# A hybrid decoder trunk on one core: the second mixer's output projection, its combines, and three shifts of order around the norms

## The chip, the core and the metric

The kernel runs on one core of a Trainium2 chip. A core has a matrix engine (TensorE, PE below), a vector engine (VectorE, DVE), an engine for activation functions (ScalarE, ACT), a general engine (GpSimd, POOL) and a queue that issues most DMA transfers (SyncE, SP). Each takes its own instructions in its own order; semaphores tie them together. The metric is the device time in microseconds (us), the median over runs. Before the change it is 2555.88 us (three runs, 2554.9 to 2557.5).

## The reference

One sequence of 1024 tokens with 1024 channels passes two layers in fp32. Each layer adds a token mixer and a SwiGLU feed-forward block to the residual stream `h`, each behind an RMS norm. Layer 0 has gated DeltaNet heads and a short convolution, layer 1 has HGRN2 heads and dilated window attention:

```
for layer in range(DEPTH):                      # DEPTH = 2
    hn = rms_norm(h, norm_mix_g[layer])
    h = h + (mixer_ab if layer % 2 == 0 else mixer_cd)(hn, ...)
    hn = rms_norm(h, norm_ffn_g[layer])
    h = h + swiglu(hn, w_gate, w_up, w_down)
return rms_norm(h, norm_final_g)

# in mixer_cd: three windows (128, 512, 2048) with dilations 1, 4, 16, four heads of 128
for p, (window, dilation) in enumerate(SWA_PATTERNS):
    o_p, lse_p = dilated_window_attention(sq[:, :, p], sk[:, :, p], sv[:, :, p], window, dilation)
wts = softmax(stack(lses), axis=-1)             # over the three windows
o_d = einsum('bthpd,bthp->bthd', stack(outs), wts)
return concatenate([o_c, o_d], axis=-1) @ w_out # 512 HGRN2 channels, 512 attention channels
```

The outputs of the three windows are weighed by a softmax over their log-sum-exps and added (the combine); together with the HGRN2 channels they go through the output projection `w_out`, 1024 by 1024.

## The kernel before

The residual and all activations lie with channels on the 128 partitions and tokens along the free axis, in two halves of 512 tokens, so a tensor of 1024 channels is 8 tiles of 128x512 per half. A product in fp32 is three matmuls: each operand is split into a high part and a remainder (`split`, lines 100 to 103: a cast on ACT, then a subtraction on DVE), and `mm3` (lines 122 to 129) adds high times high (L127), and the two mixed products (L128, L129). An output tile over 8 channel tiles k thus takes 24 matmuls of 512 columns.

Weights are read in units of 128x1024 by `wload`: a DMA into a raw buffer (`raw`, two of them), then the split into one of four units (`ring`, tag `w`). PSUM has three sets of banks: two under `psg`, three under `psu`, three under `psm`.

`out_proj` (from line 1258) is the output projection of one half. It reads the eight tiles of the concatenated mixer output from DRAM (`cat`, into `cin`), splits them, and then computes eight outputs d in pairs: two weights are loaded, one output goes to `psu`, the other to `psg`, over all k in a given order. For layer 1 that order is 0, 1, 2, 4, 5, 6, 3, 7: the last of the HGRN2 tiles and of the attention heads come last. Each output is added to the residual (L1274), squared for the next norm (`piece`: ACT square at L184, sum `acc` on POOL at L188), and stored.

The class `Trunk` holds the norm. `sums` (L200) adds the squares over partitions by small matmuls with a tile of constants; the result `rows` is taken to SBUF by DVE (L203); `inverse` transposes it on PE (L208), DVE copies it (`v`, L210), POOL raises it to the power -1/2 (`r`, L215). `spread` (L239) brings it to all partitions by transposes, and `scale` (L249) multiplies. `rms` is `sums` followed by `inverse`.

The attention part of `mixer_cd` works through four heads and, for each, three windows. The outputs of windows 1 and 2 go to DRAM (`scr_o`); with the third comes `combine` (from line 2274) for a head and a half: it fetches the two tiles (`cm0`, `cm1`, one buffer each), works out the weights on DVE with one exponential on ACT (L2285 to L2296), multiplies each of the three tiles on ACT in four pieces by a per-token weight (L2300), adds on DVE (L2302), and, two steps later, transposes the sum on PE (L2307) into `psu`; a copy on ACT and a DMA take it to `cat`, tile 4 + head. The last head's tile for a half is the projection's operand k=7.

`Local` is layer 1's input projection, with products over sums and differences of channel and token halves. `early` prepares its first weights, `turn` runs the second half's norm while the first products run; `prepared` makes the high part of a weight at once and gives back a function that makes the low part (L312, L313). `silu2` (L783 to L787) computes SiLU with a tanh on ACT and one DVE instruction, and a store follows through `out`; `self.adds` is a queue of closures for DVE, which `flush` runs a step later.

In the main loop, `out_proj` runs as a generator for half 0 and half 1. In half 1, after the second output (d == 1), `tr.rms(0)` forms half 0's norm, and after the third `norm_first` applies it.

Some sections are written under a manual schedule, in which the order in the code is the order on the engines. Elsewhere the Tile scheduler orders instructions by priority, which follows the order of the code, and by estimated readiness; `tc.high_priority(offset=n)` moves an instruction up by n. So an edit there can shift other instructions on each engine too.

Of the kernel before, what the change touches and what calls it, by code (L numbers as in the profile page):

```python
# [16 lines left out]
MULT, ADD, SUB, MAX, MIN = ALU.mult, ALU.add, ALU.subtract, ALU.max, ALU.min  # L17

P = 128
T_LEN = 1024  # L20
DM = 1024
KT = DM // P
# [33 lines left out]
def hybrid_trunk_kernel(ctx: ExitStack, tc: tile.TileContext, x_t, w_all, w_down, w_ba, vecs, c_f, c_i, c_rope, out):  # L56
    nc = tc.nc
    V, S, G, T = nc.vector, nc.scalar, nc.gpsimd, nc.tensor
# [31 lines left out]
    def psg():  # L90
        return ps.tile([P, HT], F32, tag="g", name="psg", bufs=2)

    def psu():
        return ps.tile([P, HT], F32, tag="u", name="psu", bufs=3)
# [5 lines left out]
    def split(hi, lo, src, eng=V):  # L100

        S.copy(hi, src)  # L102
        eng.tensor_tensor(lo, src, hi.bitcast(F32), op=SUB)  # L103

    def unit():

        return ring.tile([P, 2, DM], F32R, tag="w", name="w", bufs=4)

    def wload(*names, ahead=0):

        us = []
        for n in names:
            us.append(unit())
            raw = ring.tile([P, DM], F32, tag="raw", name="raw", bufs=2)
            with tc.high_priority(offset=ahead):
                dma(raw, w_all[W_AT[n]])
            split(us[-1][:, 0, :], us[-1][:, 1, :], raw)
        return us

    def wk(w, i):  # L120

        return tuple(w[i][:, z, :].rearrange("p (k c) -> p k c", k=KT) for z in range(2))
# [8 lines left out]
    def hk(hn, z, k):  # L131

        return hn[k // KH][z][:, k % KH, :]

    def proj(w, hn, order=range(KT), o=None, first=True, last=True):
        o = psu() if o is None else o
        mm3(o, [(w[0][:, k, :], w[1][:, k, :], hk(hn, 0, k), hk(hn, 1, k)) for k in order], first, last)
        return o
# [604 lines left out]
    class Local(Up):  # L743
# [36 lines left out]
        def turned(self, f):  # L780
            return PAIRS[f][0] is not None

        def silu2(self, d, x):  # L783

            th = self.right.tile([P, HT], F32, tag="sw", name="th", bufs=2)
            S.activation(th, x, AF.Tanh, scale=0.5)
            V.scalar_tensor_tensor(d, th, 1.0, x, op0=ADD, op1=MULT)  # L787

        def bounds(self):

# [74 lines left out]
        def add22(self, f):  # L865
            c = self.c22.pop(f)
            if self.turned(f):
                b = self.c22[f] = psm()
                V.tensor_tensor(b, c, self.z[f], op=ADD)
            else:  # L870
                V.tensor_tensor(c, c, self.z[f], op=ADD)
                self.silu2(c, c)
                self.out(f, 1, 1, c)

        def rope22(self, f):
            if f in self.c22:
# [21 lines left out]
        def rope21(self, f):  # L898
            x = self.x.pop(f)
            if self.turned(f):  # L900
                self.rope(f, 1, 0, x)
            else:
                z = self.right.tile([P, HT], F32, tag="z", name="z", bufs=3)
                self.silu2(z, x)
                self.out(f, 1, 0, z)
                self.flush()

        def end12(self, f, b22):
            self.prod(self.z[f], f, "s4", b22, first=False)
# [100 lines left out]
        def early(self, hx):  # L1010

            def sub(eng, dst, x, y):
                eng.tensor_tensor(dst, x, y, op=SUB)

            xa = hx.tile([P, 2, DM], F32, tag="hn", name="xa", bufs=6)
            xu = hx.tile([P, 2, DM], F32R, tag="hn", name="xu", bufs=6)
            u0, g0 = (ring.tile([P, DM], F32, tag="raw", name="raw", bufs=2) for _ in range(2))
            dma(g0, self.source("g", 0))
            for i, kind in enumerate("gu"):
                dma(xa[:, i, :], self.source(kind, 1))  # L1020
            dma(u0, self.source("u", 0))
            w2 = self.raw("g", 2, True)
            ga, sa = xa[:, 0, :], xa[:, 1, :]
            self.part_a(0, g0)
            self.part_a(1, ga)
            V.tensor_tensor(sa[:, HT:], sa[:, :HT], sa[:, HT:], op=ADD)
            sub(V, sa[:, :HT], sa[:, HT:], ga[:, :HT])
            split(xu[:, 0, :], xu[:, 1, :], sa)
            self.named(1, xu, "s2", "s1")
            self.part_a(2, w2)  # L1030
            s = self.sums(g0, u0)
            sub(G, u0[:, :HT], g0[:, :HT], u0[:, :HT])
            sub(G, g0[:, HT:], g0[:, HT:], s[:, :HT])
            low = self.prepared(0, s, "s2", "s1")
            self.begun = ga, sa, w2, u0, g0, low

        def turn(self, tr, row, b11, b21, hx, close, left, right):

            def sub(eng, dst, x, y):
                eng.tensor_tensor(dst, x, y, op=SUB)  # L1040

            ga, sa, w2, u0, g0, low = self.begun
            self.p1(0, b11)
            parts = tr.sums(1)
            y = self.y[0] = psg()
            self.prod(y, 0, "a12", b21, last=False, ks=(0,))
            dg = tr.inverse(*parts)
            low()
            self.prod(y, 0, "a12", b21, first=False, ks=(1, 2, 3))
            pb = tr.spread(dg)  # L1050
            self.p1(1, b11)
# [29 lines left out]
            low = self.prepared(0, u0, "s3", "a22")  # L1081
# [8 lines left out]
            low = self.prepared(0, g0, None, "s4")  # L1090
# [14 lines left out]
            low = self.prepared(2, sa, "s2", "s1")  # L1105
# [7 lines left out]
            low = self.prepared(1, u1, "s3", "a22")  # L1113
# [21 lines left out]
            low = self.prepared(1, s, None, "s4", us)  # L1135
# [13 lines left out]
            self.end12(1, b22)  # L1149
            self.add12(1)  # L1150
            self.s = self.sums(a, b)
            while self.stores:
                self.flush()
            self.p7(2, t3)
            self.a, self.b = a, b
# [104 lines left out]
    def out_proj(name, cat_d, tr, src, order, half, hp):  # L1260
        qs = {}
        for k in order:
            if k // KH not in qs:
                qs[k // KH] = quarter()
            f = hp.tile([P, HT], F32, tag="m", name="cin", bufs=4 - layer)
            dma(f, cat_d[k])
            split(hk(qs, 0, k), hk(qs, 1, k), f)
        tr.begin(half, src)
        for d0 in range(0, KT, 2):
            w = wload((name, d0), (name, d0 + 1))  # L1270
            for i in range(2):
                o = proj(wk(w, i), qs, order, psg() if i else psu())
                h = tr.at(half, d0 + i)
                V.tensor_tensor(h, h, o, op=ADD)  # L1274
                tr.piece(half, d0 + i, alone=half == 1)
                tr.save(half, d0 + i, hd[2 * layer][half])
                yield
# [606 lines left out]
    def mixer_cd(hn, hp, qkd, wv):  # L1884
# [6 lines left out]
        with ExitStack() as es:  # L1891
# [382 lines left out]
            def combine(h, g, ol, sums):  # L2274

                t, st = [ol], [sums]
                for p in range(2):
                    a = tl(f"cm{p}", (4, 132))
                    dma(a[:, :, 0:P + 2],
                        scr_o[h, p, g * HT:(g + 1) * HT].rearrange("(j i) d -> i j d", i=P)[:, :, 0:P + 2])  # L2280
                    t.append(a)
                    st.append(a[:, :, P:P + 2])
                yield
                mx, dn, w3, tmp = tl("mx", (4,)), tl("dn", (4,)), tl("w3", (3, 4)), tl("tmp4", (4,))
                V.tensor_tensor(mx, st[0][:, :, 0], st[1][:, :, 0], op=MIN)  # L2285
                V.tensor_tensor(mx, mx, st[2][:, :, 0], op=MIN)
                for p in range(3):
                    V.tensor_tensor(w3[:, p, :], st[p][:, :, 0], mx, op=SUB)
                S.activation(w3, w3, AF.Exp, scale=-1.0)
                for p in range(3):  # L2290
                    d = dn if p == 0 else tmp
                    V.tensor_tensor(d, w3[:, p, :], st[p][:, :, 1], op=MULT)
                    if p:
                        V.tensor_tensor(dn, dn, tmp, op=ADD)
                V.reciprocal(tmp, dn)
                V.tensor_tensor(w3, w3, tmp[:, None, :].to_broadcast([P, 3, 4]), op=MULT)  # L2296
                for p in range(3):
                    for j in range(4):
                        x, w = t[p][:, j, 0:P], w3[:, p, j:j + 1]
                        S.activation(x, x, AF.Copy, scale=w)  # L2300
                    if p:
                        V.tensor_tensor(ol[:, :, 0:P], ol[:, :, 0:P], t[p][:, :, 0:P], op=ADD)  # L2302
                yield
                yield
                o = psu()
                for j in range(4):
                    T.transpose(o[:, j * P:(j + 1) * P], t[0][:, j, 0:P], ident)  # L2307
                go = tl("sw", bufs=2)
                S.copy(go, o)
                dma(catd[g][4 + h], go)  # L2310
# [86 lines left out]
    tr = Trunk(es)  # L2397
# [64 lines left out]
    first = [[u], []]  # L2462
# [35 lines left out]
    for layer in range(2):  # L2498
# [14 lines left out]
        tr = Trunk(es)  # L2513
        row = R_FFN + layer * KT
        for half in range(NH):
            steps = out_proj(("abo", "cdo")[layer], cat[layer][half], tr, residual[half],
                             ((4, 5, 6, 7, 0, 1, 2, 3), (0, 1, 2, 4, 5, 6, 3, 7))[layer], half, hp)
            for d, _ in enumerate(steps):
                if half == 1 and d == 1:
                    dg = tr.rms(0)  # L2520
                if half == 1 and d == 2:
                    b1 = norm_first(tr, row, dg)
        mes.close()
# [11 lines left out]
        with ExitStack() as fes:  # L2535
            tr = Trunk(es)
# [98 lines left out]
```

## Time and profile before

| | |
|---|---|
| median of three runs | 2555.88 us |
| profiled execution, whole | 2557.52 us |
| its span in the trace | 2555.5 us |
| mean granted PE clock | 0.996 |
| PE busy | 2516.3 us, 98% |
| DVE busy | 1694.8 us, 66% |
| ACT busy | 1088.6 us, 43% |
| POOL busy | 651.1 us, 25% |
| moved by DMA | 451.48 MB, 177 GB/s |

The profile comes from one execution. Busy time is the time in which an engine has an instruction in work; PE's matmuls overlap, so the count of starts in a stretch says more of PE than its busy time. The granted clock is 1.00 where PE runs at its full rate. A row of the timeline reads: start in the span, duration, engine, line, operation, output and inputs with their shapes, count, and in brackets the idle time of the engine before it with what ended it. The places of the change lie as follows in the span: layer 0's output projection around 420 to 520 us, layer 1's input projection from about 1110, the last attention heads and layer 1's output projection between 1740 and 1960 us.

### The profile page before, as it was taken

Reading aid. Unit: us, or ns where it says so; the run is one execution under the profiler, and the core shown is the slowest. Engines: PE = TensorE matmul, PEld = TensorE weight load, DVE = VectorE, ACT = ScalarE, POOL = GpSimd, SP = SyncE. Lnnn points to the kernel's source line nnn. Section 1 sums busy time; section 2 is a strip of 40 time slices with the busy share of each in tenths; the row PEclk is TensorE's granted clock in tenths of the full one; section 3 lists DMA queues with packets and bytes.
Section 4 is the critical chain, followed back from the end, with each engine's and each line's share of the span. In section 5 each row is a group of like instructions: output and inputs, shape, how many; then the busy total and the mean of one; then the engine's idle time right before and its main releaser. Section 6 shows DMA issues by size and latency. Waiting matters only on the chain.

```text
span 2555.5 us, 37524 instructions
## 1 busy us (share of the span) xinstructions
PE 2516.3 (98%) x13957; PEld 2086.8 (82%) x13957; DVE 1694.8 (66%) x2849; ACT 1088.6 (43%) x1859; POOL 651.1 (25%) x557
## 2 busy tenths in 40 slices
PE   9999999999999999999999999999899999999998
PEld 7888888888888888878888888878778888888887
DVE  8887786685655565568787765666568565666554
ACT  5422113443333344334676534456634333334442
POOL 0111111343333300033566310000033433330001
PEclk9999999999999999999999999999999999999999
DMA  4435457235556688633344544576652455668853
GB/s 158 156 120 167 129 159 258 106 102 183 182 189 215 204 302 276 197 128 132 128 142 148 184 132 139 154 204 192 197 173 87 165 190 188 201 219 284 279 175 124
DMA packets 281174, 451.48 MB, mean 177 GB/s; under 512 B 49152, under 2 KB 137760, under 8 KB 280736
## 3 DMA queue, kind: packets, MB, share of 16 engines
q1 hardware_dynamic: 280992, 449.10, 53.7%
q8 instruction: 109, 1.79, 0.3%
q14 instruction: 73, 0.60, 0.1%
HBM read 304.74 MB, written 144.26 MB: 176 GB/s over the span
## 4 chain that ended last, share of the span: by engine, by line
PE 80%; DVE 7%; ACT 3%; DMA 2%; issue 2%; POOL 1%; SPq 0%; DVEq 0%; POOLq 0%; ACTq 0%
PE psu L127 15%; PE psu L129 15%; PE psu L128 15%; PE psg L129 6%; PE psg L127 6%; PE psg L128 6%; PE psm L127 4%; PE psm L129 4%; PE psm L128 4%; DVE h L249 1%; PE psm L2247 1%; DMA cm<-scr_o 1%; DVE w L103 1%; DVE h L616 1%; DVE w L313 1%
## 5 line engine op out<-in xcount | busy, mean ns | idle before, releaser
L103 DVE TENSOR_TENSOR w<-raw,w 128x1024 fp32r<-128x1024 f32 x323 | 384.6, 1192 | 133.0 <-ACT w L102 132.4
L102 ACT CAST w<-raw 128x1024 fp32r<-128x1024 f32 x323 | 309.1, 958 | 266.1 <-PE psu L129 130.6
L127 PE MATMUL psu<-hnh,w 128*128 128x512 f32 x832 | 331.2, 398 | 0.2 <-ACT w L102 0.2
L129 PE MATMUL psu<-hnh,w 128*128 128x512 f32 x832 | 325.3, 391 | 0.5 <-DVE w L103 0.5
L128 PE MATMUL psu<-hnl,w 128*128 128x512 f32 x832 | 324.9, 390 | 0.0
L188 POOL TENSOR_TENSOR acc<-acc,sq 128x512 f32<-128x512 f32 x52 | 79.2, 1523 | 535.1 <-ACT sq L184 535.0
L129 PEld LDWEIGHTS psu<-hnh,w 128*128 128x128 f32 x832 | 156.3, 188 | 34.0 <-DVE w L103 1.0
L127 PEld LDWEIGHTS psu<-hnh,w 128*128 128x128 f32 x832 | 156.6, 188 | 32.9 <-ACT w L102 0.7
L128 PEld LDWEIGHTS psu<-hnl,w 128*128 128x128 f32 x832 | 156.7, 188 | 30.8
L326 POOL TENSOR_TENSOR ws<-raw 128x512 f32<-128x512 f32 x54 | 73.2, 1356 | 398.2 <-DMA raw<-in_dram 274.7
L103 DVE TENSOR_TENSOR w<-ws,w 128x1024 fp32r<-128x1024 f32 x51 | 66.7, 1309 | 119.8 <-ACT w L102 119.8
L103 DVE TENSOR_TENSOR hidq<-hr,hidq 128x1024 fp32r<-128x1024 f32 x72 | 82.0, 1141 | 78.4 <-ACT hidq L102 78.2
L102 ACT CAST hidq<-hr 128x1024 fp32r<-128x1024 f32 x72 | 70.3, 980 | 104.2 <-DMA hr<-ts 63.4
L127 PE MATMUL psm<-hidq,w 128*128 128x512 f32 (+1 forms) x275 | 106.1, 386 | 0.0
L128 PE MATMUL psm<-hidq,w 128*128 128x512 f32 (+1 forms) x275 | 105.8, 385 | 0.0
L129 PE MATMUL psm<-hidq,w 128*128 128x512 f32 (+1 forms) x275 | 105.8, 385 | 0.0
L846 POOL TENSOR_TENSOR sw<-sw,rope 128x512 f32<-128x512 f32 x48 | 71.7, 1493 | 93.5 <-ACT sw L845 60.3
L127 PE MATMUL psu<-t3h,w 128*128 128x512 f32 x240 | 93.9, 391 | 0.9 <-ACT u L389 0.9
L127 PE MATMUL psu<-t4h,w 128*128 128x512 f32 x240 | 93.7, 391 | 0.6 <-ACT c L396 0.6
L417 POOL TENSOR_TENSOR hid<-hid,c 128x512 f32<-128x512 f32 x44 | 62.1, 1411 | 125.1 <-ACT hid L416 124.9
L332 POOL TENSOR_TENSOR raw<-raw,ws 128x512 f32<-128x512 f32 x51 | 78.9, 1547 | 58.7 <-DVE w L103 57.5
L129 PE MATMUL psu<-t4h,w 128*128 128x512 f32 x240 | 93.4, 389 | 0.0
(536 smaller groups left out, 6702.6 us busy)
## 6 DMA issues: line engine op xcount, KB each, us to landing
raw<-in_dram SPq DMA_DIRECT2D x227, 512.0 KB, 4.1
sd<-in_dram SPq DMA_DIRECT2D x44, 512.0 KB, 3.8
hid<-hid SPq DMA_DIRECT2D x88, 256.0 KB, 2.9
sd<-sd SPq DMA_DIRECT2D x44, 512.0 KB, 3.1
hr<-ts SPq DMA_DIRECT2D x40, 512.0 KB, 4.5
raw<-sd SPq DMA_DIRECT2D x40, 512.0 KB, 4.5
qk<-z SPq DMA_DIRECT2D x52, 256.0 KB, 2.5
hd<-h SPq DMA_DIRECT2D x48, 256.0 KB, 2.9
```

The costliest lines, as they stand in the source:

```text
L102: S.copy(hi, src)
L103: eng.tensor_tensor(lo, src, hi.bitcast(F32), op=SUB)
L127: T.matmul(o, lh, rh, start=first and i == 0, stop=False, **kw)
L128: T.matmul(o, lh, rl, start=False, stop=False, **kw)
L129: T.matmul(o, ll, rh, start=False, stop=last and i == n - 1, **kw)
L188: (eng or G).tensor_tensor(a, a, q, op=ADD)
L249: V.scalar_tensor_tensor(h, h, vec[:, row + k:row + k + 1], pb, op0=MULT, op1=MULT)
L313: later(lambda: V.tensor_tensor(u[:, 1, c], src[:, c], u[:, 0, c].bitcast(F32), op=SUB))
L326: G.tensor_tensor(s[:, HT:], b[:, :HT], b[:, HT:], op=ADD)
L332: G.tensor_tensor(a[:, HT:], a[:, HT:], s[:, :HT], op=SUB)
L417: G.tensor_tensor(h, h, self.c22.pop(f), op=MULT)
L846: G.tensor_tensor(sw, sw, self.table[:, 1, t], op=MULT)
```

## The change

There are five edits.

A. `out_proj`: for layer 1 and half 0 the first four outputs are opened at once. Four weights are loaded, the four outputs run over the first seven k in two `psu` and two `psg` banks, and then each is closed with k=7. The other outputs, and the other halves, go in pairs as before.

B. `Local.early` and `turn`: of the second and third weight (f = 1, 2) only the high part is made in `early`; their low parts on DVE stand, with a third one that stood there already, behind the inverse of the second half's norm sums.

C. Main loop: `tr.rms(0)` runs with priority raised by 60, in both layers. In the resulting order the sums of half 0 (L200) stand behind 10 matmuls of half 1 in layer 0 and behind 9 in layer 1, where they stood behind 48; the transpose of the rows stands 3 matmuls behind them, the spread where it stood.

D. `combine`: the tile `ol` is scaled by one DVE instruction of 128x512 with the weights broadcast, in place of four ACT activations; the two additions come after it. The two fetched tiles are scaled on ACT as before.

E. `Local.silu2`: the DVE instruction after the tanh and its store go into the queue `self.adds` and so run a step later.

Line numbers after the change are higher by 3 at `silu2`, by 7 at the projection's addition (L1281) and by 7 or 8 in `combine` (the additions L2310, the scaling of `ol` L2308, the transposes L2315).

```diff
@@ silu2
-        def silu2(self, d, x):
+        def silu2(self, f, half, d, x):
             th = self.right.tile([P, HT], F32, tag="sw", name="th", bufs=2)
             S.activation(th, x, AF.Tanh, scale=0.5)
-            V.scalar_tensor_tensor(d, th, 1.0, x, op0=ADD, op1=MULT)
+            self.flush()
+            def add():
+                V.scalar_tensor_tensor(d, th, 1.0, x, op0=ADD, op1=MULT)
+                self.out(f, 1, half, d)
+            self.adds.append(add)
...
@@ early
-            self.part_a(1, ga)
+            low1 = self.prepared(1, ga, "a11", "a12")
...
-            self.part_a(2, w2)
+            low2 = self.prepared(2, w2, "a11", "a12")
...
-            self.begun = ga, sa, w2, u0, g0, low
+            self.begun = ga, sa, w2, u0, g0, (low1, low, low2)
@@ turn
             dg = tr.inverse(*parts)
-            low()
+            for low in lows:
+                low()
@@ out_proj
-        for d0 in range(0, KT, 2):
-            w = wload((name, d0), (name, d0 + 1))
-            for i in range(2):
-                o = proj(wk(w, i), qs, order, psg() if i else psu())
+        for d0, n in ((0, 4), (4, 2), (6, 2)) if layer and not half else ((0, 2), (2, 2), (4, 2), (6, 2)):
+            w = wload(*((name, d0 + i) for i in range(n)))
+            os_ = [None] * n
+            if n == 4:
+                os_ = [proj(wk(w, i), qs, order[:7], psg() if i % 2 else psu(), last=False) for i in range(n)]
+            for i, o in enumerate(os_):
+                o = proj(wk(w, i), qs, order[7 * (n // 4):], o or (psg() if i else psu()), first=n < 4)
@@ combine
-                for p in range(3):
+                for p in range(1, 3):
                     for j in range(4):
                         x, w = t[p][:, j, 0:P], w3[:, p, j:j + 1]
                         S.activation(x, x, AF.Copy, scale=w)
-                    if p:
-                        V.tensor_tensor(ol[:, :, 0:P], ol[:, :, 0:P], t[p][:, :, 0:P], op=ADD)
+                V.tensor_tensor(ol[:, :, 0:P], ol[:, :, 0:P], w3[:, 0, :, None].to_broadcast([P, 4, P]), op=MULT)
+                for p in range(1, 3):
+                    V.tensor_tensor(ol[:, :, 0:P], ol[:, :, 0:P], t[p][:, :, 0:P], op=ADD)
@@ main loop
                 if half == 1 and d == 1:
-                    dg = tr.rms(0)
+                    with tc.high_priority(offset=60):
+                        dg = tr.rms(0)
```

More of the change, by code (lines that the diff above doesn't have):

```diff
@@ L871, in add22 @@
                 V.tensor_tensor(c, c, self.z[f], op=ADD)
-                self.silu2(c, c)
-                self.out(f, 1, 1, c)
+                self.silu2(f, 1, c, c)
         def rope22(self, f):
@@ L903, in rope21 @@
                 z = self.right.tile([P, HT], F32, tag="z", name="z", bufs=3)
-                self.silu2(z, x)
-                self.out(f, 1, 0, z)
-                self.flush()
+                self.silu2(f, 0, z, x)
         def end12(self, f, b22):
@@ L1040, in sub @@
                 eng.tensor_tensor(dst, x, y, op=SUB)
-            ga, sa, w2, u0, g0, low = self.begun
+            ga, sa, w2, u0, g0, lows = self.begun
             self.p1(0, b11)
@@ L1151, in turn @@
             self.s = self.sums(a, b)
-            while self.stores:
+            while self.stores or self.adds:
                 self.flush()
```

## The prediction

> **What bounds the kernel now.** I read the page's totals first, then the busy time by stretches, then what TensorE (PE) waited for, and last the timeline round each place that the change touches.
>
> ```profile
> span 2555.5 us, 37524 instructions
> ```
> ```profile
> PE 2516.3 (98%) x13957; PEld 2086.8 (82%) x13957; DVE 1694.8 (66%) x2849; ACT 1088.6 (43%) x1859; POOL 651.1 (25%) x557
> ```
> ```profile
> 1860.00:1960.00 100.00, 96.58 (x443) 77.26 (x442) 76.83 (x81) 46.42 (x56) 33.38 (x18) 1.00 0.34 110
> 1960.00:2500.00 540.00, 540.00 (x2384) 447.30 (x2383) 319.77 (x392) 207.20 (x268) 144.39 (x106) 1.00 0.62 211
> 1826.70:1830.10 3.40, 3.37 (x11) 2.88 (x12) 2.00 (x4) 1.60 (x3) 0.00 (x0) 0.56 0.39 128
> 1137.10:1140.50 3.40, 3.40 (x11) 2.54 (x10) 0.94 (x1) 0.00 (x0) 3.07 (x2) 0.54 0.02 5
> ```
> ```profile
> PE psg L127 <- ACT hnh L102: 7.0, 1, 7.0
> PE psm L2179 <- DVE stat L2186: 2.8, 1, 2.8
> PE psm L208 <- DVE rows L203: 2.3, 2, 1.7
> PE psm L200 <- ACT sq L184: 1.9, 1, 1.9
> PE psu L2307 <- DVE ol L2302: 1.8, 2, 1.0
> ```
> The columns of the stretches are length, then busy time and count of PE, its weight loads, VectorE (DVE), ScalarE (ACT) and GpSimd (POOL), then the granted clock, the DMA share and GB/s. PE is busy 98% of the span. In its densest stretch it starts 2384 matmuls in 540.00 us: 0.2265 us each, my price for one matmul of 512 columns. The change adds none and removes none, so it can only win back idle PE time or lost clock. The waits on its path are 7.0 (the projection for its eighth operand), 1.8 (the combines), 1.9 and 2.3 (norm sums). After the waits of 7.0 and 1.9 the granted clock is 0.56 and 0.54 for 3.40 us: 3.40 x 0.44 = 1.5 us and 3.40 x 0.46 = 1.6 us more. The 100 us round layer 1's second-half sums hold their 1.73 us wait (row below) at clock 1.00, so that one cost no clock. [...]
>
> **Parts A and D: output projection of layer 1, half 0, and the combines that feed it.**
> ```profile
> 1804.68 0.66 PE L2307 MATMUL psu<-cf,ol 128*128 128x128 f32 x4 [1.00 <-DVE ol L2302]
> ...
> 1816.94 0.66 PE L2307 MATMUL psu<-cf,ol 128*128 128x128 f32 x4 [0.77 <-DVE ol L2302]
> ...
> 1826.73 0.79 PE L127 MATMUL psg<-hnh,w 128*128 128x512 f32 x1 [7.04 <-ACT hnh L102]
> ```
> ```profile
> 1810.34 1.22 DVE L103 TENSOR_TENSOR w<-raw,w 128x1024 fp32r<-128x1024 f32 x1
> ...
> 1812.27 0.17 DVE L2296 TENSOR_TENSOR w<-w,tmp 128x12 f32<-128x12 f32 x1
> 1815.02 0.69 DVE L2302 TENSOR_TENSOR ol<-ol,cm 128x512 f32<-128x512 f32 x1 [2.58 <-ACT cm L2300]
> ```
> ```profile
> 1812.54 1.28 ACT L2300 ACTIVATE ol<-ol,w 128x128 f32<-128x128 f32 x4 [2.69 <-DVE w L2296]
> 1813.72 2.44 ACT L2300 ACTIVATE cm<-cm,w 128x128 f32<-128x128 f32 x8
> ...
> 1823.74 2.43 ACT L2300 ACTIVATE cm<-cm,w 128x128 f32<-128x128 f32 x8
> ```
> ```profile
> L2072 DVE TENSOR_TENSOR e<-e,rr 128x512 f32<-128x512 f32 x1 | 0.7, 693 | 1.2 <-POOL rr L2071 1.2
> ```
> A combine weighs three attention outputs, adds them, transposes the sum on PE and writes it to DRAM; the projection reads it back. The buffers "cm" exist once, so the combines form a chain: each fetches only when the one before has added. The transposes at 1816.94 (head 3, half 0) feed operand k=7, whose cast arrives 9.8 us later, at 1826.73; PE has run out of work 7.04 us before.
>
> D: from the weights (1812.27) to the adds ACT works 4 activations on ol (1812.54 to 1813.72 where the next begins: 1.2 us) and then 8 on cm. Those 4 go; DVE does the same in one instruction of 512 columns, 0.69 us by the nearest row of this broadcast form, while ACT is on the first cm. So each link is 1.2 us shorter. Head 3's first combine is the third link that shifts: 3.6 us. DVE's new order also takes one weight split (1810.34, 1.22 us) and one operand split, some 0.65 us, out of this chain: 1.9 us. Transposes then come at 1816.94 - 5.5 = 1811.4. Bounds: 1813.3 (links alone), 1810.5 (all foreign work that moves counted).
>
> A: in the changed order only 7 projection matmuls stand before these transposes, before there are 33: PE gets there 26 x 0.2265 = 5.9 us sooner, 1816.17 - 5.9 = 1810.3, and waits 1.1 us (0.77 before). Behind the transposes come 31 matmuls (7.0 us), the transposes of the last combine, 42 + 4 matmuls and then 12 that close the four outputs. The last combine's sum would be ready, by its cm activations, at 1823.74 + 2.43 + 0.7 = 1826.9; four links and 1.9 us make it 1826.9 - 6.7 = 1820.2. PE arrives at 1811.4 + 0.6 + 7.0 = 1819.0 and waits 1.2. Operand k=7 is there at 1811.4 + 9.8 = 1821.2; PE wants it at 1820.2 + 0.6 + 46 x 0.2265 = 1831.2: the wait of 7.0 us and its 1.5 us of clock are gone, with 10 us to spare. The closings end at 1831.2 + 12 x 0.2265 = 1833.9. What is late next: all four weight units come free only there, and the low part of the fifth weight (1.22 us) stands on DVE behind two additions of 0.7 us; I count 0.5 us of PE wait, so 1834.4. Before, the fifth output began at 1830.10 + 10.80 = 1840.9: this stretch of the trace is
>
> ```profile
> 1830.10:1840.90 10.80, 10.80 (x49) 8.94 (x48) 5.19 (x8) 5.54 (x9) 0.00 (x0) 1.00 0.84 259
> ```
> full at clock 1.00. A and D together: 1834.4 - 1840.9 = -6.5 us. Bounds: -4.6 with 1813.3; -10.3 if nothing takes the place of 7.0 + 1.5 + 1.8.
>
> **Part B: low parts behind the norm's sums (layer 1's input projection).**
> ```profile
> 1130.45 2.32 DVE L103 TENSOR_TENSOR w<-xa,w 128x1024 fp32r<-128x1024 f32 x1
> 1132.70 1.21 DVE L103 TENSOR_TENSOR w<-raw,w 128x1024 fp32r<-128x1024 f32 x1
> ...
> 1140.83 0.75 DVE L249 SCALAR_TENSOR_TENSOR h<-h,vec,psm 128x512 f32<-128x512 f32 x1 [2.79 <-PE psm L239]
> ```
> Two splits, 3.5 us, stand on DVE ahead of the addition whose square PE waits 1.9 us for. Behind the inverse they fall into DVE's idle 2.79 us, and 0.7 us or more of them does not fit. Away go 1.9 and 1.6 us of clock: -3.5 at most. From there DVE, which carries the norm's scalings, has as much to do as before, so part comes back. Bounds -3.5 and 0; I take -2.0, nearer the wait than the clock.
>
> **Part C: the first half's sums moved forward.**
> ```profile
> 453.89 1.74 POOL L188 TENSOR_TENSOR acc<-acc,sq 128x512 f32<-128x512 f32 x1 [1.15 <-ACT sq L184]
> ...
> 1867.99 1.62 POOL L188 TENSOR_TENSOR acc<-acc,sq 128x512 f32<-128x512 f32 x1 [2.54 <-ACT sq L184]
> ```
> ```profile
> 451.97 0.39 PE L127 MATMUL psu<-hnh,w 128*128 128x512 f32 x1
> ...
> 1864.35 0.50 PE L129 MATMUL psu<-hnh,w 128*128 128x512 f32 x1 [0.53 <-DVE w L103]
> ...
> 1878.28 0.33 PE L208 MATMUL psm<-cf,rows 128*128 128x128 f32 x1 [1.73 <-DVE rows L203]
> ```
> Before, the sums stood behind 48 matmuls of the second half, in the changed order behind 10 (layer 0) and 9 (layer 1). Layer 0: PE arrives at 451.97 + 2.3 = 454.2, POOL's last square sum ends at 455.6: a new wait of 1.4 us. Layer 1: the addition came late because DVE waited for weights; with it at its place POOL ends about 1.0 us after PE arrives; as the trace stands PE would arrive at 1864.35 + 7 x 0.23 = 1866.0 and wait until 1869.6, 3.6 us. The transpose of the rows, three matmuls later, now waits perhaps 0.3 us in each layer; the 1.73 us wait goes. Sum: 1.4 + 1.0 + 0.6 - 1.7 = +1.3. Bounds: -1.7 (sums in time) and 1.4 + 3.6 + 1.6 + 1.6 - 1.7 = +6.5 (both waits with half clock). What is queued behind is PE's whole stream; the spread stays where it was, so an earlier inverse gains nothing.
>
> **Part E: the last step of the SiLU one tick later.**
> ```profile
> L787 DVE SCALAR_TENSOR_TENSOR z<-th,psu 128x512 f32<-128x512 f32 x4 | 2.7, 682 | 0.6 <-ACT th L786 0.6
> ```
> Eight instructions of this kind and their stores (SyncE's queue) go later; DVE loses an idle wait of 0.6 us that no PE wait answers to. Cover: PE. 0, and 0.7 us if a PSUM bank comes free too late.
>
> **Sum**: -6.5 - 2.0 + 1.3 + 0 = -7.2. The profiled execution took 2557.52 us (2.0 of it outside the span), 1.64 above the median of the three runs; 2550.3 against it is 2548.7 against the median.
>
> **Rivals.**
> 1. The wait changes place. PE takes its instructions in order: in the trace the 7.04 us are idle although two more outputs' matmuls follow. If the combine chain is not set by ACT but by its fetches, D is worth nothing: the last sum stays at 1826.9, PE waits there instead, and 1826.9 + 0.6 + 13.1 + 0.5 = 1841.1 is where the fifth output began. A and D 0; the rest -0.7: 2555.2. For it: one link took 12.2 us (1804.68 to 1816.94), ACT's part in it only 3.7. Against: the fetch cannot start before the adds, which the 1.2 us delay. [...]
> 2. Part C at its upper bound, +6.5 instead of +1.3: 2553.9. For it: half clock after 1.9 us. Against: none after 1.73.
> 3. Slower: weights starve. Four units come free at once, two raw buffers refill them. PE uses a weight in 24 x 0.2265 = 5.4 us, so two buffers hold as long as a fetch and two splits (1.2 us each, as at 1810.34) take under 10.9 us, a fetch under 8.5. If the fetches collide with stores and operands and take 11 us, each of the twelve weights left loses (11 + 2.4 - 10.9) / 2 = 1.25: +15, less the 7.2: 2563.7. Against:
> ```profile
> raw<-in_dram SPq DMA_DIRECT2D x227, 512.0 KB, 4.1
> ```
> half of the limit; for it DMA at 0.84 in 1830.10 to 1840.90.
> 4. More: every named wait vanishes, -10.3 - 3.5 - 1.7 = -15.5: 2540.4. Against: transposes that stand 26 matmuls earlier must wait for something.
>
> **How the numbers follow.** Forecast 0.50, rivals 0.14, 0.09, 0.15, 0.12. A measurement here tells 0.2% (5.1 us, below 2550.8) from no change. Of the forecast's own range, 2544 to 2553, 0.43 lies below that and 0.07 within; with rival 4 faster is 0.55. Same: 0.07 + 0.14 + 0.09 = 0.30. Slower 0.15. The range 2541 to 2557 leaves out most of rival 4 and rival 3. The likeliest case gives 2548.7.
>
> **What would show it.** A, D: no wait of L127 for hnh; the ACT activations on ol gone; transposes of head 3 at about 1805 to 1820, waits of about 1 us. B: the wait L200 for sq gone, clock full at the spread. C: L200 waiting for POOL's acc near 454 and 1860. Wrong if the waits for ol reach 5 us, if L103 or L102 of weights stops PE after the closings, or if C's waits bring half clock.

## The result and the profile after the change

The changed kernel takes 2551.43 us (median of 15 runs, 2549.18 to 2555.55), the kernel before 2557.04 us (15 runs beside them, 2554.46 to 2558.74). The ratio is 0.9982 with a 95% interval of 0.9974 to 0.9990: faster by 0.18%, some 4.6 us, where 7.2 us were forecast. It lies inside the stated range, and right at the 0.2% that the prediction set between "faster" and "same": 0.18% by the ratio over all runs, 0.22% by the two medians. The profiled execution took 2553.74 us, its span is 2551.7 us.

What PE waited for in the whole span of the changed kernel (total, times, longest, in us), the first rows:

```profile
PE psm L200 <- POOL acc L188: 4.5, 2, 3.3
PE psm L2186 <- DVE stat L2193: 3.4, 2, 1.8
PE psu L129 <- issue: 2.2, 1, 2.2
PE psm L2254 <- DVE pt L2237: 2.1, 1, 2.1
```

The 7.0 us for `hnh` that led this list are gone, and so are the 1.9 us for `sq`. At its head stands a wait that was not there: the norm sums for POOL's sum of squares, 1.3 us in layer 0 and 3.3 us in layer 1. (The row with "issue" is an idle stretch at 1722 us, far from every edit; in the execution of before it is 0.96 us.)

The stretches that answer to those of before, with the same columns:

```profile
1110.00:1180.00 70.00, 69.26 (x319) 55.68 (x318) 59.90 (x67) 31.91 (x45) 25.71 (x13) 1.00 0.27 98
1740.00:1860.00 120.00, 111.43 (x595) 93.17 (x593) 73.49 (x210) 68.07 (x176) 9.71 (x7) 1.00 0.71 226
1860.00:1960.00 100.00, 96.90 (x436) 78.25 (x437) 77.30 (x82) 45.03 (x55) 34.04 (x19) 0.97 0.29 96
1862.18:1867.88 5.70, 5.70 (x21) 4.15 (x22) 4.34 (x6) 3.04 (x3) 1.93 (x1) 0.50 0.51 198
```

The clock is full at part B's place (1110 to 1180) and at A's and D's (1740 to 1860). The loss is in the third row, where before it was 1.00: the 5.7 us behind the new wait of layer 1 ran at half clock (the fourth row), which costs up to 2.9 us.

PE's timeline at the places of C and A:

```profile
455.74 0.43 PE L200 MATMUL psm<-acc,onesn 128*32 128x128 f32 x8 [1.26 <-POOL acc L188]
...
1810.57 0.60 PE L2254 MATMUL psm<-vp,pt 128*128 128x128 f32 x3 [2.13 <-DVE pt L2237]
...
1820.87 0.63 PE L2315 MATMUL psu<-cf,ol 128*128 128x128 f32 x4 [1.18 <-DVE ol L2310]
...
1835.22 0.50 PE L129 MATMUL psu<-hnh,w 128*128 128x512 f32 x1
...
1862.18 0.65 PE L200 MATMUL psm<-acc,onesn 128*32 128x128 f32 x8 [3.26 <-POOL acc L188]
```

And the chain that ends in the last of these waits, back from it (start, us, what):

```profile
1849.01 8.00 DMA raw<-in_dram
...
1857.09 1.06 ACT w L102
...
1858.17 1.23 DVE w L103
1859.40 0.61 DVE h L1281
...
1860.09 0.64 ACT sq L184
...
1860.87 1.27 POOL acc L188
```

The eighth output's addition (L1281) stood on DVE behind the low part of a weight of the second half, whose fetch took 8.00 us. PE had closed that output and begun the next; its matmul ahead of the sums started at 1858.5.

### The profile page after: what moved, and what is told of

Read it like the earlier page. It is cut to its first block, busy times and chain, and to the rows that moved or that the text cites. A ratio compares the mean times of both kernels' runs of the same rounds, so it can differ in the third digit from the quotient of the medians.

```text
span 2551.7 us, 37524 instructions
## 1 busy us (share of the span) xinstructions
PE 2515.9 (99%) x13957; PEld 2084.5 (82%) x13957; DVE 1697.0 (67%) x2857; ACT 1079.0 (42%) x1827; POOL 649.5 (25%) x557
## 5 line engine op out<-in xcount | busy, mean ns | idle before, releaser
L103 DVE TENSOR_TENSOR w<-raw,w 128x1024 fp32r<-128x1024 f32 (+1 forms) x322 | 380.9, 1185 | 133.0 <-ACT w L102 132.0
L102 ACT CAST w<-raw 128x1024 fp32r<-128x1024 f32 (+1 forms) x322 | 308.1, 958 | 269.3 <-PE psu L129 134.4
L127 PE MATMUL psu<-t3h,w 128*128 128x512 f32 x240 | 93.8, 391 | 1.2 <-ACT u L389 1.2
L127 PE MATMUL psu<-t4h,w 128*128 128x512 f32 x240 | 93.7, 391 | 0.5 <-ACT c L396 0.5
L128 PE MATMUL psu<-t4l,w 128*128 128x512 f32 x240 | 93.4, 389 | 0.0
L129 PE MATMUL psu<-t3h,w 128*128 128x512 f32 x240 | 93.4, 389 | 0.0
```

The lines of the kernel that those rows point to most:

```text
L127: T.matmul(o, lh, rh, start=first and i == 0, stop=False, **kw)
L128: T.matmul(o, lh, rl, start=False, stop=False, **kw)
L129: T.matmul(o, ll, rh, start=False, stop=last and i == n - 1, **kw)
```

## The experiments

Theory 1: D makes the combine chain shorter, B takes 1.9 us and its clock away, C costs what PE waits for POOL's sum. The rival to its first part: opening four outputs at once is what covers operand k=7. Theory 2 came after the first four runs: part of what is won at 1842 us is given back at 1860, because the second half's first weights come late.

All kernels run the same 13957 matmuls, so the time from the n-th to the m-th can be compared between traces. The table gives the difference from before, in us, for four stretches of PE's instructions (named by their times before). Each is of one execution; the ratios are of all runs.

| kernel | ratio to before, 95% interval | 404 to 493 | 1114 to 1171 | 1785 to 1842 | 1860 to 1931 |
|---|---|---|---|---|---|
| changed (A to E) | 0.9982, 0.9974 to 0.9990 | +1.8 | -2.7 | -5.2 | +2.7 |
| D alone | 0.9981, 0.9970 to 0.9991 | +1.0 | 0.0 | -6.8 | +3.6 |
| A alone | 1.0003, 0.9995 to 1.0012 | +0.6 | -0.1 | +2.6 | -3.3 |
| A and D | 0.9976, 0.9967 to 0.9985 | +0.8 | 0.0 | -6.6 | -1.3 |
| all but C | 0.9969, 0.9958 to 0.9981 | +0.4 | -2.7 | -6.7 | +3.0 |
| C alone | 1.0014, 1.0005 to 1.0023 | +2.1 | -1.1 | +1.2 | +1.4 |
| B alone | 0.9992, 0.9983 to 1.0001 | +0.8 | -2.7 | +0.5 | -2.5 |
| E alone | 0.9999, 0.9990 to 1.0008 | +0.4 | 0.0 | +0.1 | -1.9 |
| C at 30 | 0.9965, 0.9953 to 0.9978 | +1.3 | -2.7 | -6.0 | -0.6 |
| all but C, early fetches | 0.9962, 0.9949 to 0.9974 | +0.2 | -2.7 | -6.9 | -2.6 |
| C at 30, early fetches | 0.9969, 0.9959 to 0.9980 | +1.5 | -2.7 | -7.1 | -0.9 |
| C at 60, early fetches | 0.9987, 0.9978 to 0.9996 | +1.3 | -2.7 | -6.2 | +2.6 |
| B, D, E, early fetches | 0.9963, 0.9950 to 0.9975 | +0.4 | -2.7 | -7.2 | -2.0 |

Single executions differ, so the columns need care. In the first, A, B, D and E change nothing and stand at 0.4 to 1.0. In the last, B alone and E alone change nothing and stand at -2.5 and -1.9: the execution of before lost some 2 us there. Of the five kernels above 0 in it, three show half clock in that stretch (0.50 in the changed kernel and in all but C, 0.51 in C alone), so a good part of this column is clock there.

**A or D.** D alone:

```diff
-                for p in range(3):
+                for p in range(1, 3):
...
+                V.tensor_tensor(ol[:, :, 0:P], ol[:, :, 0:P], w3[:, 0, :, None].to_broadcast([P, 4, P]), op=MULT)
```

> Before plus edit D alone (ol scaled on DVE). In the order of its instructions the transposes of head 3 already stand where the changed kernel has them (7 projection matmuls, transposes, 31, transposes), and k=7 is needed only 21 matmuls of d0 later: 31 + 4 + 21 = 56 matmuls or 12.7 us behind the first of these transposes, against the 9.8 us that k=7 takes to come back. Theory 1 (D shortens the combine chain and with it moves the transposes; A only adds slack): no wait of 7 us, 1.5 us of clock back, about -6 us in the stretch 1790 to 1841, ratio 0.9976. Rival (opening four outputs at once is what covers k=7): a wait of 2 us or more for hnh remains and half or less of the gain, -3 us or less.

A alone (the loop of `out_proj` as in the change, nothing else):

```diff
+        for d0, n in ((0, 4), (4, 2), (6, 2)) if layer and not half else ((0, 2), (2, 2), (4, 2), (6, 2)):
```

> Before plus edit A alone (four outputs opened at once). In its order 33 projection matmuls still stand ahead of head 3's first transposes and 10 between them and the second, the tenth with k=7. Theory 1: the wait for k=7 stays at about 7 us, with its half clock; the time is that of before, ratio 0.999 to 1.001. Rival (A covers k=7): the wait is gone, about -6 us, ratio 0.9976.

Both:

> Before plus A and D. Theory 1: the same as D alone within 1 us in that stretch, -6 to -7 us, ratio 0.9974. Rival: clearly more than D alone, by 3 us or more.

D alone wins 6.8 us in the stretch, A alone is 2.6 us longer, the two together win 6.6. PE's waits from 1789 to 1842 us, D alone:

```profile
PE psm L2247 <- DVE pt L2230: 2.5, 1, 2.5
```

and A alone, to 1850 us, the first rows:

```profile
PE psg L127 <- ACT hnh L102: 6.9, 1, 6.9
PE psu L2310 <- DVE ol L2305: 1.5, 2, 0.8
PE psg L127 <- ACT w L102: 0.9, 1, 0.9
PE psu L129 <- DVE w L103: 0.8, 1, 0.8
```

With A alone the wait for k=7 stays, and behind it come 0.9 and 0.8 us for the weights after the four closings, and half clock for 4.5 us (a matmul of 512 columns lasts 0.63 us there and 0.39 behind it) where before had 3.0. The order says why the wait stays: 33 matmuls still stand ahead of head 3's first transposes, and the tenth of the ten between them and the second ones needs k=7. With D alone the order has 7, then 31, and k=7 is first needed after 21 matmuls more. That D shortens the sum can be read from DVE, where the weights of the combine are followed by its last addition. Before (the weights at 1812.27 stand in the prediction) and changed:

```profile
1816.19 0.69 DVE L2302 TENSOR_TENSOR ol<-ol,cm 128x512 f32<-128x512 f32 x1 [0.48 <-ACT cm L2300]
```
```profile
1808.41 0.17 DVE L2303 TENSOR_TENSOR w<-w,tmp 128x12 f32<-128x12 f32 x1
1808.62 0.69 DVE L2308 TENSOR_TENSOR ol<-ol,w 128x512 f32<-128x512 f32 x1
...
1810.43 1.48 DVE L2310 TENSOR_TENSOR ol<-ol,cm 128x512 f32<-128x512 f32 x2
```

It took 4.6 us before and takes 3.5 now, 1.1 less (forecast 1.2). The scheduler, which orders by when it expects an operand, then puts the transposes earlier itself; D alone has no other edit that could do it. How much of the 6.8 us is the shorter chain and how much the moved order was not separated: one brings the other. That A and D together have the better ratio than D alone (0.9976, 0.9981) is within the intervals.

**C.** The changed kernel without it:

```diff
-                    with tc.high_priority(offset=60):
-                        dg = tr.rms(0)
+                    dg = tr.rms(0)
```

> The changed kernel without edit C (sums without priority, in both layers). Theory 1 (C costs its new waits for POOL's sum): the waits of PE for acc are gone (1.3 us in layer 0; 3.3 us and 1.5 us of half clock in layer 1), the wait for the rows of 1.7 us is back in layer 1: about 4.5 us less than the changed kernel, some 2547, ratio to before 0.9963. Rival (the earlier sums pay elsewhere, or PE merely waits at another place): the time of the changed kernel within 1 us.

and C alone, on the kernel before:

> Before plus edit C alone. Theory 1: PE waits for POOL's acc 1.3 us in layer 0 and about 3.5 us in layer 1, perhaps with 1.5 us of half clock, and not for the rows (1.7 us): +1.3 in layer 0, +1 to +3.4 in layer 1, ratio 1.000 to 1.0018. Theory 2 adds that in layer 1 it is a wash where the rows would have waited more than 1.7 us. Rival (the earlier sums help): ratio under 0.9995.

C alone is slower, by 0.14%, some 3.6 us. Without it the changed kernel is faster, by ratio 0.9969 to 0.9982 or 0.13%, though by the medians (2549.48 to 2551.43) only 2 us, not the 4.5 expected; the two intervals overlap, so it is C alone, with its interval above 1, that shows the loss. Layer 0 is as forecast: its wait for `acc`, 1.3 us in the changed kernel and in C alone, is gone. In layer 1, in these executions, one wait only takes the place of another. PE's waits from 1845 to 1885 us, all but C:

```profile
PE psm L208 <- DVE rows L203: 3.5, 1, 3.5
```

and DVE there:

```profile
1864.48 1.23 DVE L103 TENSOR_TENSOR w<-raw,w 128x1024 fp32r<-128x1024 f32 x1 [3.08 <-ACT w L102]
1865.62 0.68 DVE L1281 TENSOR_TENSOR h<-h,psg 128x512 f32<-128x512 f32 x1
1866.22 0.28 DVE L203 TENSOR_SCALAR rows<-psm 128x128 f32<-128x128 f32 x1
```

The rows stand behind a weight's low part that waited 3.08 us, as the addition did with C. Behind both waits the clock is halved: for 5.7 us with C (above), and for 5.4 without it:

```profile
1866.56:1871.99 5.43, 5.43 (x14) 4.28 (x15) 1.30 (x2) 1.21 (x2) 2.76 (x2) 0.50 0.82 241
```

**The weights.** In the run of all but C, the raw buffers of these weights come free at 1837.2 and 1841.0, when the splits before them end. SyncE's queue there:

```profile
1837.79 0.32 SPq L243 DMA_DIRECT2D hd<-h  x1
1838.16 2.35 SPq L168 DMA_DIRECT2D h<-hd  x5
1841.63 0.32 SPq L243 DMA_DIRECT2D hd<-h  x1
1841.99 0.43 SPq L168 DMA_DIRECT2D h<-hd  x1
1842.52 0.95 SPq L116 DMA_DIRECT2D raw<-in_dram  x2
```

The two fetches are issued at 1842.5 and 1843.1, behind two stores that wait for their outputs, and behind the residual's loads. In the next kernel they are moved ahead:

```diff
-            w = wload(*((name, d0 + i) for i in range(n)))
+            w = wload(*((name, d0 + i) for i in range(n)), ahead=100 if layer and half and not d0 else 0)
```

> The changed kernel without C, and with the fetches of the first two weights of layer 1's second half given priority, so that on SyncE's queue they stand ahead of two stores and eight residual loads, and start when their raw buffers come free (1837 and 1841 in the run without C) instead of at 1842.5 and 1843.1. Theory 2 (what is given back behind the first four outputs comes from these weights, late by the order on SyncE's queue; DVE waits for them, and the addition, the square sum and the rows stand behind them): the fifth wait for weights round 1850 is gone, the wait for the rows, 3.5 us without C, falls under 2 us, the stretch 1860 to 1931 is 3 us or more shorter than in the run without C; about 2546, ratio 0.9955. Rival (the DMA engines are full there): the fetches take as much longer as they start earlier, and the time is that of the run without C within 1 us.

The wait for the rows falls from 3.5 to 0.4 us:

```profile
PE psm L208 <- DVE rows L203: 0.4, 1, 0.4
```

In this execution the buffers come free at 1841.4 and 1845.2 and the fetches go out at 1842.4 and 1845.3. The first takes 3.9 us, where it took 5.4 without the change, so the rival (they take as much longer) has fallen. The last column goes from +3.0 to -2.6, and the time is 2547.83 us, ratio 0.9962. So the stretch is 5.6 us shorter in these two executions, as theory 2 said, the half clock included. In the ratio (0.9969 to 0.9962) the gain is smaller and within the intervals, so it is not shown in the time: not every execution loses 3 us there; that of A and D, with the same order at that place, lost none.

**C at a lower priority, and C with weights in time.** Offset 30 in place of 60:

> The changed kernel with C's priority raised by 30 instead of 60: the sums stand behind some 24 matmuls of the second half instead of 9 or 10. Theory 1 (C's cost is that PE arrives before POOL's square sum): layer 0's wait of 1.3 us is gone, layer 1's wait for acc is under 1 us; ratio 0.996 to 0.997, 1.3 to 4.5 us less than the changed kernel. Rival: the time of the changed kernel.

2547.91 us, ratio 0.9965: no wait for `acc` in layer 0, none in layer 1, where the rows cost 1.4 us. But layer 0's stretch is still 1.3 us longer than before, where the kernels without C stand at 0.2 to 1.0. The order tells the rest: the eight small matmuls of the sums are now strewn in three places between projection matmuls.

```profile
457.55 0.41 PE L200 MATMUL psm<-acc,onesn 128*32 128x128 f32 x4
457.89 0.49 PE L127 MATMUL psg<-hnh,w 128*128 128x512 f32 x1
458.32 0.41 PE L200 MATMUL psm<-acc,onesn 128*32 128x128 f32 x2
458.65 0.49 PE L128 MATMUL psg<-hnl,w 128*128 128x512 f32 x1
459.08 0.41 PE L200 MATMUL psm<-acc,onesn 128*32 128x128 f32 x2
```

From the start of the projection matmul ahead of them (457.23) to that of the second one behind them (459.75) are 2.5 us, for four projection matmuls that take 0.9 by themselves: 1.6 us. In one group (all but C, 462.37 to 463.38, two projection matmuls) the same eight add 0.6 us.

With the early fetches as well, at 30 and at 60:

> The changed kernel with the early fetches of the run before and C's priority at 30: the sums behind 24 matmuls in both layers. Theory 2 (late weights make the sums late in layer 1): no wait for acc in layer 1 and under 1 us for the rows; some 2547, ratio 0.9960 to 0.9965, no difference from the early fetches without C of over 1 us. Rival (C at a moderate priority gains by itself): 1 us or more under the early fetches alone.

> The changed kernel, C at 60 as it is, with the early fetches. Theory 2: with the weights in time the addition and the square sum come in time too, and layer 1's wait for acc falls from 3.3 us to 1 us or less, without half clock; layer 0's wait of 1.3 us stays; 2 to 4 us less than the changed kernel, ratio 0.9966. Rival (the wait in layer 1 is POOL's own length behind the last output): it stays above 2 us.

At 60 the expectation missed: the wait for `acc` in layer 1 is 4.3 us, not 1. DVE of that kernel:

```profile
1856.71 1.23 DVE L103 TENSOR_TENSOR w<-raw,w 128x1024 fp32r<-128x1024 f32 x1 [5.10 <-ACT w L102]
1857.85 0.68 DVE L1281 TENSOR_TENSOR h<-h,psg 128x512 f32<-128x512 f32 x1
```

With two weights fetched earlier, the scheduler put the third one's low part ahead of the eighth output's addition, and that one waits 5.10 us. The mechanism is the same, an addition behind a late weight; the early fetch moves it on by one weight. The rival's number came (above 2 us), but not its cause: POOL's last sum took 1.70 of the 4.3 us. At 30 the expectation missed too: PE still waits 1.3 us for `acc`, and the ratio, 0.9969, lies above the 0.9960 to 0.9965 expected. So C gains nothing once the weights are early, and loses at 60 (0.9987 against 0.9962).

**B, E, and the version without A and C.**

> Before plus edit B alone. Theory: the wait of 1.9 us for the square and the half clock behind it are gone in the stretch 1114 to 1171, -2.7 us as in the changed kernel, ratio 0.9990. Rival (VectorE's chain behind the norm takes it back further on): the stretch to 1440 gives back 1.5 us or more, ratio 0.9995 to 1.

> Before plus edit E alone. Theory: nothing on PE's path, ratio 0.9995 to 1.0005. Rival: a bank of PSUM comes free a step later and PE waits 0.7 us or more in the stretch 1171 to 1400, ratio above 1.0005.

> B, D and E with the early fetches, without A and C. Theory 1 (D moves the transposes, A only adds slack): the stretch 1785 to 1842 as short as with A, 6 to 7 us under before, no wait for hnh; about 2548, ratio 0.9962. Rival (A carries 1 us or more): 1 to 3 us slower than the early fetches with A.

B alone gives the 2.7 us of the changed kernel and no more than 0.4 us of it back up to 1400 us; its ratio is 0.9992, with an interval up to 1.0001. E is neutral, 0.9999. B, D and E with the early fetches, without A and C, take 2545.83 us, ratio 0.9963: as good as with A (0.9962), and 1.9 per mille better than the change as made (the intervals just meet, at 0.9974 to 0.9975). These two have the lowest ratios of the study.

## Why the prediction was right or wrong

**A and D, forecast -6.5:** the size is right (-5.2 to -7.2 in nine kernels that have D), and the steps mostly are. The fifth output began at 1834.5, forecast 1834.4; that this fits so closely is partly luck, since this execution was 0.8 us ahead of before at 1785 already, and from there it won 5.6 up to the fifth output. One link of the combine chain became 1.1 us shorter, forecast 1.2. The last transposes wait 1.18 us, forecast 1.2. The weight stall behind the closings is 0.3 us, forecast 0.5 (its third matmul, 1835.22, starts 0.50 us after the second instead of 0.23). The 1.1 us at head 3's first transposes came as 2.13 us one step earlier, at `pt`, a copy that now stands on DVE behind the weights of the combine and the new scaling of `ol`. What failed is the step "A: in the changed order only 7 projection matmuls stand before these transposes": the order is as said, but it is D's doing. A alone leaves the wait of 6.9 us, D alone removes it. Rival 1, with D worth nothing, has fallen.

**B, forecast -2.0:** measured -2.7. Two terms were mis-sized and in part made up for each other. The half clock was priced at 1.6 us; C alone, which keeps the wait of 1.88 us at clock 1.00, is 1.1 us shorter than before there, so it cost 1.1. Of 1.9 and 1.1 then only 0.3 came back, where the forecast let 1.5 of 3.5 go.

**C, forecast +1.3:** mis-sized, about +3.5 by C alone. Layer 0's wait was 1.26 us (forecast 1.4) and brought no half clock (1.00 for the 3.40 us behind it). In layer 1 the term "with it at its place POOL ends about 1.0 us after PE arrives" failed: the addition was not at its place, since the second half's weights were late still, and the wait was 3.26 us with half clock (0.50) behind it, up to 2.9 us more, near the bound of 3.6 and 1.6. Half clock behind C's waits was one of the prediction's own signs of being wrong. The 0.3 us at each transpose of the rows did not come. That bound is rival 2's, which had named the price but not the cause. And the 1.7 us for the rows that C takes away is itself only one draw: without C that wait is nothing (A alone) to 3.5 us (all but C).

**E, forecast 0:** right.

**Not in the sum:** what D wins at 1842 us moves PE nearer to the weights. Rival 3 named the right resource, but as a shortage of transfer: what held the weights back was first their place on SyncE's queue, as the early fetches show. The fetches were slow as well, 6.1 and 8.0 us side by side in the changed kernel against a median of 4.1; how much of the lateness is queue and how much transfer was not separated. The two misses, C's second half and this, can account for the 2.6 us between forecast and result, but no run shows that split, and the interval is 4 us wide.

## What to carry to other kernels

Where a scheduler orders by expected readiness, an edit that shortens a chain also moves the instructions at its end: test each edit alone before crediting one. Before raising the priority of a sum, look at what its last operand stands behind on the other engine: in all but C, DVE waited 3.08 us for a late weight, the addition and the rows stood behind that and have nothing to do with it, and PE waited 3.5 us for the rows. When a stall goes, look at the queue that issues the next transfers: here two fetches stood behind stores that had to wait, with their buffers free.

## What the runs showed of the hardware

Whether an idle stretch halves the clock is not settled by its length alone. In the kernel before the wait of 1.88 us at 1135 us was followed by half clock (0.54 from 1137.10 to 1140.50, in the prediction); in C alone a wait of 1.88 us at the same place was not, which is the -1.1 of that row in the table:

```profile
1137.00:1140.40 3.40, 3.33 (x21) 2.24 (x13) 1.59 (x3) 0.22 (x1) 1.88 (x1) 1.00 0.18 69
```

The same wait for `pt` kept the clock in the changed kernel (2.13 us idle, longer than the 1.88 that lost it before):

```profile
1810.50:1813.90 3.40, 3.33 (x21) 2.87 (x22) 2.53 (x4) 2.57 (x5) 0.00 (x0) 1.00 0.70 190
```

and halved it in all but C with the early fetches (2.01 us idle):

```profile
1808.30:1811.70 3.40, 3.38 (x15) 3.08 (x16) 2.48 (x3) 2.04 (x4) 0.00 (x0) 0.54 0.69 196
```

What else settles it was not shown. So half clock, priced at 1.6 us in the prediction, came behind the wait of 1.9 us in the execution of before and not in that of C alone.
